# Gating a decoder's expert mixer in rounds of eight tokens instead of four, with single one-hot tiles and another order of ACT and DVE

## The chip, the cores and the metric

The kernel runs on one core of a Trainium2 chip. The metric is the device time of one execution in microseconds (us), as the median of several runs. The engines are TensorE (PE, whose weight loads are listed apart as PEld), VectorE (DVE), ScalarE (ACT), GpSimd (POOL) and SyncE (SP, which here issues the weight transfers). Each engine works through its own queue in order; work on different engines is tied by semaphores.

## The reference

Two decoder layers on 256 tokens of width 1024. Each layer has a token mixer (two kinds of attention, left out here) and a retrieval over 16384 single-neuron experts, and the change is in the second. A token has 8 heads of 16 chosen experts; an expert's index is a pair (i, j) of two 128-way indices.

```python
def expert_block(args):
    tb, eb, gb = args                 # tokens, chosen experts, gates
    act = gelu(einsum('td,ted->te', tb, expert_u[eb]))
    return einsum('te,ted->td', gb * act, expert_v[eb])
```

The kernel doesn't gather the experts. It computes the activations of all 16384 for all tokens, multiplies them by a dense matrix of gates (zero for experts that a token did not choose), and multiplies the result by all of expert_v.

## The kernel before, in words

Everything is in fp32 or in pairs of fp32r halves: a weight block of 128 x 1024 (512 KB) is fetched by SP (`fetch`), ACT rounds it to `hi` (line 90), DVE takes the rest `lo` (line 91), and a product is three matmuls (lines 119 to 121). Blocks come in one fixed order (`plan`). `weights` hands out block n and has block n + 2 cut on the spot (`ahead`); `hi`, `lo` and the raw blocks have three buffers each. The order of instructions in each queue is that of the program text, written out by hand.

A layer's expert part (`peer`, line 666) has these stages. First come queries, scores and the top-16 selection, with 48 of the 128 projections by expert_u beside them (M_PRE = 48, tile `bufa`: for each j one chunk of 128 i x 256 tokens). The selection leaves for each token, in 128 partitions (8 heads x 16), the two indices and the gate cut in three bf16 parts; the tiles are `tT` (lines 953 to 963). Then comes the gating stage, and last `sum_b` (line 155), which multiplies all 128 gated chunks by expert_v; `lhs` cuts a chunk into two halves for it (lines 715 and 716).

The gating stage (lines 723 to 756) does two things together: the other 80 projections (tile `bufb`), and the dense gates. For a token, a one-hot tile compares the i index with 0..127, another the j index (`one_hots`, line 769, against the constant `iotax`); the second is multiplied by the three gate parts (`gated`, line 778). Three matmuls a token then sum a 128 x 128 matrix of gates in PSUM (`dense`, line 788). Tiles hold tokens in adjacent pairs. A round has TB = 4 tokens: four DVE instructions for one-hots, twelve matmuls into one PSUM bank. `apply` (line 791) multiplies these gates into the chunks that are already there: on DVE into `bufa` (line 795) and the J - 48 projected chunks of `bufb` (line 797), and then ACT copies the gates of the chunks still to come into `bufb` (line 799). A later projection J finds gates for the tokens of earlier rounds in its chunk: ACT puts their Gelu into a tile `g` (line 751), that of the other tokens straight into the chunk (line 753), and DVE multiplies `g` in (line 755, "g product" below).

There are 64 rounds and one more, with one or two projections each, so that 80 are done by the end. Within a round the text has: the one-hots of the next round, the projection (with the cut of a later block by ACT and DVE), the gated one-hots of the next round, `apply` for the round before, `dense` for this one, g and Gelu. One-hots and gated one-hots have two buffers, save the j one-hots with one.

At the start of the kernel, 14 matmuls on a constant tile `ones` run while x is fetched (lines 281 to 285). After the first projections of layer 0, thirty small matmuls on `iotax` write a bank that nobody reads (lines 401 to 407). `norm_t` squares x on ACT into the tile `hT[0]` as scratch (lines 213 to 215), in four pieces of 512 columns, scales an identity to `diag` (line 243), and cuts the transposed result into `hT` on ACT (line 251) and DVE (line 252).

Of the kernel before, what the change touches and what calls it, by code (L numbers as in the profile page):

```python
# [9 lines left out]
F32 = mybir.dt.float32  # L10
F32R = mybir.dt.float32r
BF = mybir.dt.bfloat16
U32 = mybir.dt.uint32
AF = mybir.ActivationFunctionType
OP = mybir.AluOpType
# [7 lines left out]
S = 256  # L23
# [8 lines left out]
NCAND = sum(RUNS)  # L32

M_PRE = 48
TB = 4
WARM = 14
NB = S // TB
TAIL = 2
# [7 lines left out]
class Kern:  # L46
# [209 lines left out]
    def build(self):  # L256
        nc, tc, i = self.nc, self.tc, self.i
        with ExitStack() as st:
# [19 lines left out]
            self.gains = const.tile([128, 2, self.depth, KT], F32, name="gains")  # L278
            nc.gpsimd.dma_start(self.gains, i["norm_g"][:, :, 0:self.depth])

            ones = const.tile([128, 128], F32, name="ones")
            nc.vector.memset(ones, 1.0)
            ps = self.bank("ps")
            for _ in range(WARM):
                nc.tensor.matmul(ps[:, 0:128], ones, ones, start=True, stop=True)
            self.iotab = const.tile([128, TOPK], BF, name="iotab")
            self.iotax = const.tile([128, TB // 2, 128, 2], BF, name="iotax")
            self.starts = const.tile([128, 2, 16], BF, name="starts")
            for l in range(self.depth):
                self.mixer(l)  # L290
# [25 lines left out]
    def constants(self, pool):  # L316

        nc, i = self.nc, self.i
        iota = pool.tile([128, 128], F32, name="iota")
        nc.gpsimd.dma_start(iota, i["c_iota"])  # L320
        s32 = pool.tile([128, 2, 16], F32, name="s32")
        nc.gpsimd.dma_start(s32, i["c_runs"])
        rel = pool.tile([33, 5], F32, name="rel")
        oh = pool.tile([33, 384], F32, name="oh")
        nc.gpsimd.dma_start(oh, i["c_bucket"])
        flip = pool.tile([128, 128], F32, name="flip")
        nc.gpsimd.dma_start(flip, i["c_flip"])
        nc.vector.memset(rel, 0.0)
        nc.gpsimd.dma_start(rel[0:32, 0:4], i["rel_bias"])
        nc.vector.memset(rel[32:33, :], 1.0)  # L330
        yield
        ps = self.bank("acc")
        nc.tensor.matmul(ps[0:5, 0:384], rel, oh, start=True, stop=True)
        er = pool.tile([5, 384], F32, name="er")
        nc.vector.tensor_scalar(er, ps[0:5, 0:384], -1.0, None, op0=OP.mult)
        nc.vector.tensor_copy(self.iotab, iota[:, :TOPK])
        for q in range(TB // 2):
            nc.vector.tensor_copy(self.iotax[:, q], iota[:, :, None].to_broadcast([128, 128, 2]))
        nc.vector.tensor_copy(self.starts, s32)
        erow = self.dram.tile([5, 384], F32, name="erow")  # L340
        nc.gpsimd.dma_start(erow, er)

        tr = pool.tile([128, 5, S], F32, name="tr")
        nc.gpsimd.dma_start(tr, bass.AP(tensor=erow.tensor, offset=erow.offset, ap=[[1, 128], [384, 5], [1, S]]))
        yield
        ts = pool.tile([128, 5, S], F32, name="ts")
        for h in range(5):
            ps = self.bank("acc")[:, :S]
            nc.tensor.matmul(ps, flip, tr[:, h], start=True, stop=True)
            nc.scalar.activation(ts[:, h], ps, AF.Copy)  # L350
        self.table = self.dram.tile([128, 5, S], F32, name="table")
        nc.gpsimd.dma_start(self.table, ts)
        yield

    def mixer(self, l):
        nc, tc, i = self.nc, self.tc, self.i
        lam_init = 0.8 - 0.6 * math.exp(-0.3 * l)
        with tc.tile_pool(name="mix", bufs=1) as mp, tc.tile_pool(name="att", bufs=1) as ap, ExitStack() as first:
# [39 lines left out]
                    nc.vector.tensor_scalar(nlam, nlam, -lam_init, None, op0=OP.add)  # L398
            first.close()
            self.ahead(self.used + 3)  # L400
            if l == 0:
                ps = self.bank("acc")
                a = self.iotax[:, 0].rearrange("p n t -> p (n t)")
                b = self.iotax[:, 1].rearrange("p n t -> p (n t)")
                for x, y in ((a[:, :128], b[:, :128]), (a[:, ::2], b[:, :128]), (a[:, :128], b[:, ::2])):
                    for _ in range(10):
                        nc.tensor.matmul(ps[:, :128], x, y, start=True, stop=True)
            tb = mp.tile([128, 5, S], F32, name="tb")
            nc.gpsimd.dma_start(tb, self.table)

# [255 lines left out]
    def peer(self, l):  # L666
        nc, tc, i = self.nc, self.tc, self.i
        with ExitStack() as st:
            sm = st.enter_context(tc.tile_pool(name="sm", bufs=1))
            pa = st.enter_context(tc.tile_pool(name="bufa", bufs=1))  # L670
            tT = [sm.tile([128, S], BF, name=f"tT{q}") for q in range(2)] + [sm.tile([128, S // 2, 3, 2], BF, name="gp")]
            bufa = pa.tile([128, M_PRE, S], F32, name="bufa")
            with tc.tile_pool(name="topk", bufs=1) as tk:
                self.norm_t(tk, self.gains[:, 1, l])
# [48 lines left out]
            with tc.tile_pool(name="wp", bufs=1) as wp:  # L723

                J = M_PRE
                hots = [self.gated(wp, 0, tT, self.one_hots(wp, 0, tT))]
                dense = []
                for b in range(NB + 1):
                    want = M_PRE + -(-(b + 1) * (NJ - M_PRE) // (NB + 1))
                    done = False  # L730
                    while J < want or not done:
                        if not done and b + 1 < NB:
                            hot = self.one_hots(wp, b + 1, tT)
                        if b == NB and not done:
                            self.apply(dense.pop(0), b - 1, bufa, bufb, J)
                            lhs(0)
                            done = True
                        ps = self.proj("uT", l, J) if J < want else None
                        if not done:
                            if b + 1 < NB:  # L740
                                hots.append(self.gated(wp, b + 1, tT, hot))
                            if b >= 1:
                                self.apply(dense.pop(0), b - 1, bufa, bufb, J)
                            if b < NB:
                                dense.append(self.dense(hots.pop(0)))
                            done = True
                        if ps is not None:
                            t0 = max(b, 0) * TB
                            if t0:
                                g = self.ring(wp, "g", [128, S], F32, 1)  # L750
                                nc.scalar.activation(g[:, :t0], ps[:, :t0], AF.Gelu)  # L751
                            if t0 < S:
                                nc.scalar.activation(chunk(J)[:, t0:], ps[:, t0:], AF.Gelu)  # L753
                            if t0:
                                nc.vector.tensor_mul(chunk(J)[:, :t0], chunk(J)[:, :t0], g[:, :t0])  # L755
                            J += 1
# [2 lines left out]
            cuts += [vq.tile([128, 2, S], F32R, name=f"cut{q}") for q in range(2, 4)]  # L759
            self.sum_b(NJ, ("v", l), lhs)  # L760

    def one_hots(self, sm, b, tT):

        nc = self.nc
        ts = slice(b * TB, (b + 1) * TB)
        shp = [128, TB // 2, 128, 2]
        o = [self.ring(sm, f"oh{q}", shp, BF, 2 - q) for q in range(2)]
        for q in range(2):
            nc.vector.tensor_tensor(o[q], self.iotax, tT[q][:, ts].rearrange("p (a b) -> p a b", b=2)[:, :, None].to_broadcast(shp),  # L769
                                    op=OP.is_equal)  # L770
        return o

    def gated(self, sm, b, tT, hot):

        og = self.ring(sm, "ohG", [128, TB // 2, 3, 128, 2], BF, 2)
        for a in range(TB // 2):
            shp = [128, 3, 128, 2]
            self.nc.vector.tensor_tensor(og[:, a], hot[1][:, a, None].to_broadcast(shp),  # L778
                                         tT[2][:, b * TB // 2 + a, :, None].to_broadcast(shp), op=OP.mult)
        return hot[0], og  # L780

    def dense(self, hots):

        oa, og = hots
        ps = self.bank("acc").rearrange("p (t c) -> p t c", c=128)
        for t in range(TB):
            for k in range(3):
                self.nc.tensor.matmul(ps[:, t], oa[:, t // 2, :, t % 2], og[:, t // 2, k, :, t % 2], start=k == 0, stop=k == 2)  # L788
        return ps

    def apply(self, ps, b, bufa, bufb, J):
        nc = self.nc
        ts = slice(b * TB, (b + 1) * TB)
        pv = ps.rearrange("p t c -> p c t")
        nc.vector.tensor_mul(bufa[:, :, ts], pv[:, :M_PRE], bufa[:, :, ts])  # L795
        if J > M_PRE:
            nc.vector.tensor_mul(bufb[:, :J - M_PRE, ts], pv[:, M_PRE:J], bufb[:, :J - M_PRE, ts])  # L797
        if J < NJ:
            nc.scalar.activation(bufb[:, J - M_PRE:, ts], pv[:, J:], AF.Copy)  # L799

    def score(self, tk, sk, q, u):

# [24 lines left out]
    def select(self, tk, tT):  # L827
# [119 lines left out]
        for tt in both:  # L947
# [2 lines left out]
                                     e[:, tt * PH:(tt + 1) * PH].rearrange("p h k -> p (h k)"))):  # L950
                nc.tensor.transpose(ps[:, q * 128:(q + 1) * 128], src, self.ident)
            yield None
            ts = slice(tt * 128, (tt + 1) * 128)
            for q in range(2):
                nc.scalar.activation(tT[q][:, ts], ps[:, q * 128:(q + 1) * 128], AF.Copy)

            rest = self.ring(tk, "rest", [128, 128], F32, 2)
            parts = [tT[2][:, tt * 64:(tt + 1) * 64, k] for k in range(3)]
            pg, r2 = [v.rearrange("p (a b) -> p a b", b=2) for v in (ps[:, 256:384], rest)]
            nc.scalar.activation(parts[0], pg, AF.Copy)  # L960
            nc.vector.tensor_sub(r2, pg, parts[0])
            nc.scalar.activation(parts[1], r2, AF.Copy)
            nc.vector.tensor_sub(parts[2], r2, parts[1])

# [79 lines left out]
```

## Time and profile before

| | us |
|---|---|
| median of 3 runs | 2120.43 |
| lowest, highest | 2120.34, 2125.4 |
| profiled execution, its own time | 2122.72 |
| its span, first to last instruction | 2120.6 |
| PE busy in the span | 2059.1 |
| DVE busy | 1479.6 |
| ACT busy | 1059.7 |

The span is what the trace covers; the profiled execution's own time lies 2.1 us above it. Busy time of an engine is the time in which it had an instruction in work. Matmuls are pipelined, one begins before the last has ended, so PE's pace is read from distances between starts. [...]

### The profile page before, as it was taken

Reading aid. Unit: us, or ns where it says so; the run is one execution under the profiler, and the core shown is the slowest. Engines: PE = TensorE matmul, PEld = TensorE weight load, DVE = VectorE, ACT = ScalarE, POOL = GpSimd, SP = SyncE. Lnnn points to the kernel's source line nnn. Section 1 sums busy time; section 2 is a strip of 40 time slices with the busy share of each in tenths; the row PEclk is TensorE's granted clock in tenths of the full one; section 3 lists DMA queues with packets and bytes.
Section 4 is the critical chain, followed back from the end, with each engine's and each line's share of the span. In section 5 each row is a group of like instructions: output and inputs, shape, how many; then the busy total and the mean of one; then the engine's idle time right before and its main releaser. Section 6 shows DMA issues by size and latency. Waiting matters only on the chain.

```text
span 2120.6 us, 37332 instructions
## 1 busy us (share of the span) xinstructions
PE 2059.1 (97%) x14594; PEld 1879.0 (89%) x14594; DVE 1479.6 (70%) x3255; ACT 1059.7 (50%) x1964; POOL 28.0 (1%) x50
## 2 busy tenths in 40 slices
PE   9999999999999999999999999999999999999998
PEld 8998999998888788888899989999888887888886
DVE  4667798777888655555566668887788885555555
ACT  5665546443333444444466655564433334444444
POOL 2000000000000000000010000000000000000000
PEclk9999999999999999999999999999999999999999
DMA  7455566544444555555555455665444445555564
GB/s 224 144 152 168 160 186 192 162 138 133 137 133 134 171 189 189 189 189 188 189 167 157 153 169 163 189 189 150 140 130 139 130 140 176 189 189 189 188 188 152
DMA packets 97393, 352.76 MB, mean 166 GB/s; under 512 B 11152, under 2 KB 11317, under 8 KB 97216
## 3 DMA queue, kind: packets, MB, share of 16 engines
q1 hardware_dynamic: 95472, 345.68, 52.4%
q0 software_dynamic: 1456, 4.18, 0.7%
q8 instruction: 114, 1.87, 0.4%
q14 instruction: 63, 0.52, 0.1%
q10 hardware_dynamic: 288, 0.52, 0.1%
HBM read 348.62 MB, written 1.71 MB: 165 GB/s over the span
## 4 chain that ended last, share of the span: by engine, by line
PE 71%; DVE 17%; ACT 8%; issue 3%; DMA 0%; POOL 0%; ACTq 0%; POOLq 0%; SPq 0%
PE acc L152 36%; PE ps L119 10%; PE ps L121 10%; PE ps L120 10%; DVE lo L91 7%; DVE ohG L778 5%; ACT hi L90 5%; ACT g L751 2%; DVE bufa L795 1%; DVE oh L769 1%; DVE bufb L797 1%; ACT bufb L753 1%; PE ps L152 1%; PE acc L788 1%; PE acc L806 1%
## 5 line engine op out<-in xcount | busy, mean ns | idle before, releaser
L91 DVE TENSOR_TENSOR lo<-raw,hi 128x1024 fp32r<-128x1024 f32 (+1 forms) x656 | 802.0, 1224 | 487.2 <-ACT hi L90 483.5
L90 ACT ACTIVATE hi<-raw 128x1024 fp32r<-128x1024 f32 (+1 forms) x656 | 696.9, 1063 | 394.7 <-PE acc L152 386.1
L119 PE MATMUL ps<-hT,hi 128*128 128x256 f32 x2784 | 799.8, 287 | 0.0
L121 PE MATMUL ps<-hT,lo 128*128 128x256 f32 x2784 | 783.8, 282 | 13.7 <-DVE lo L91 13.6
L120 PE MATMUL ps<-hT,hi 128*128 128x256 f32 x2784 | 784.4, 282 | 0.0
L152 PE MATMUL acc<-hi,cut 128*128 128x512 f32 x2048 | 562.5, 396 | 6.0 <-ACT cut L715 6.0
L121 PEld LDWEIGHTS ps<-hT,lo 128*128 128x128 f32 x2784 | 524.9, 189 | 19.7 <-DVE lo L91 19.1
L119 PEld LDWEIGHTS ps<-hT,hi 128*128 128x128 f32 x2784 | 523.2, 188 | 3.9 <-issue 3.7
L120 PEld LDWEIGHTS ps<-hT,hi 128*128 128x128 f32 x2784 | 523.7, 188 | 0.3
L152 PEld LDWEIGHTS acc<-hi,cut 128*128 128x128 f32 x2048 | 386.1, 189 | 96.6 <-ACT cut L715 6.4
L152 PE MATMUL acc<-lo,cut 128*128 128x512 f32 x1024 | 322.3, 395 | 0.0
L152 PEld LDWEIGHTS acc<-lo,cut 128*128 128x128 f32 x1024 | 192.8, 188 | 45.9
L799 ACT ACTIVATE bufb<-acc 128x312 f32<-128x312 f32 (+42 forms) x128 | 38.9, 304 | 370.6 <-DVE bufb L797 311.6
L788 PE MATMUL acc<-ohG,oh 128*128 128x128 bf16 x1536 | 117.2, 219 | 26.1 <-DVE ohG L778 26.1
L788 PEld LDWEIGHTS <-oh 128*128 128x128 bf16 x1536 | 95.3, 97 | 41.0 <-issue 30.1
L778 DVE TENSOR_TENSOR ohG<-oh,gp 128x768 bf16<-128x768 bf16 x256 | 130.7, 552 | 0.1
L755 DVE TENSOR_TENSOR bufb<-bufb,g 128x4 f32<-128x4 f32 (+25 forms) x156 | 45.6, 293 | 74.7 <-ACT g L751 74.7
L769 DVE TENSOR_TENSOR oh<-iotax,tT 128x512 bf16<-128x512 bf16 x256 | 96.5, 419 | 0.0
L690 ACT ACTIVATE bufa<-ps 128x256 f32<-128x256 f32 x96 | 37.1, 386 | 112.1 <-PE ps L121 112.0
L716 DVE TENSOR_TENSOR cut<-bufb,cut 128x256 fp32r<-128x256 f32 x160 | 66.9, 418 | 0.0
L715 ACT ACTIVATE cut<-bufb 128x256 fp32r<-128x256 f32 x160 | 64.3, 402 | 0.0
L753 ACT ACTIVATE bufb<-ps 128x240 f32<-128x240 f32 (+47 forms) x158 | 46.0, 291 | 7.5 <-PE ps L121 7.5
(240 smaller groups left out, 1413.1 us busy)
## 6 DMA issues: line engine op xcount, KB each, us to landing
raw<-uT SPq DMA_DIRECT2D x256, 512.0 KB, 3.7
raw<-expert_v SPq DMA_DIRECT2D x256, 512.0 KB, 3.6
raw<-wA SPq DMA_DIRECT2D x64, 512.0 KB, 3.6
raw<-wQ SPq DMA_DIRECT2D x32, 512.0 KB, 3.7
raw<-wV SPq DMA_DIRECT2D x16, 516.0 KB, 4.3
raw<-wO SPq DMA_DIRECT2D x16, 512.0 KB, 3.8
raw<-w_out SPq DMA_DIRECT2D x16, 512.0 KB, 4.0
tb<-table POOLq DMA_DIRECT2D x2, 640.0 KB, 5.8
```

The lines of the kernel that those rows point to most:

```text
L90: nc.scalar.activation(hi[:, :w], raw[:, :w], AF.Copy)
L91: nc.vector.tensor_sub(lo[:, :w], raw[:, :w], hi[:, :w].bitcast(F32))
L119: self.nc.tensor.matmul(ps, ah, bh, start=first and q == 0, stop=False)
L120: self.nc.tensor.matmul(ps, ah, bl, start=False, stop=False)
L121: self.nc.tensor.matmul(ps, al, bh, start=False, stop=last and q == n - 1)
L152: self.nc.tensor.matmul(ps[:, :width], a, b[:, g * width:(g + 1) * width], start=first and n == 0, stop=last and n == 2)
L715: nc.scalar.activation(a[:, 0], chunk(n), AF.Copy)
L716: nc.vector.tensor_sub(a[:, 1], chunk(n), a[:, 0].bitcast(F32))
L753: nc.scalar.activation(chunk(J)[:, t0:], ps[:, t0:], AF.Gelu)
L769: nc.vector.tensor_tensor(o[q], self.iotax, tT[q][:, ts].rearrange("p (a b) -> p a b", b=2)[:, :, None].to_broadcast(shp), op=OP.is_equal)
L778: self.nc.vector.tensor_tensor(og[:, a], hot[1][:, a, None].to_broadcast(shp), tT[2][:, b * TB // 2 + a, :, None].to_broadcast(shp), op=OP ...
L788: self.nc.tensor.matmul(ps[:, t], oa[:, t // 2, :, t % 2], og[:, t // 2, k, :, t % 2], start=k == 0, stop=k == 2)
```

## The change

- Rounds have eight tokens (32 and one more), with two or three projections each. The projections of a round are steps: after the first comes `dense` for this round, after the second `apply` for this round and then the one-hots of the next.
- `one_hots` makes both kinds of index one-hots for eight tokens in one DVE instruction of 2048 elements a partition, and the gated ones in one of 3072; both tiles have one buffer. The index and gate tiles `tT` are laid out by rounds for it; ACT and DVE write them in the selection with as many instructions as before.
- `dense` is 24 matmuls in a row, into two banks.
- `apply` has ACT copy first, for both banks, and then the DVE products.
- `ones` is no tile of its own but the first 128 columns of `hT[0]`; `iotax` has one copy instead of two; the thirty matmuls on it are gone.

```diff
-TB = 4
+TB = 8
...
-            ones = const.tile([128, 128], F32, name="ones")
+            ones = self.hT[0].rearrange("p k t -> p (k t)")[:, :128].bitcast(F32)
...
-            if l == 0:
-                ps = self.bank("acc")
-                a = self.iotax[:, 0].rearrange("p n t -> p (n t)")
-                b = self.iotax[:, 1].rearrange("p n t -> p (n t)")
-                for x, y in ((a[:, :128], b[:, :128]), (a[:, ::2], b[:, :128]), (a[:, :128], b[:, ::2])):
-                    for _ in range(10):
-                        nc.tensor.matmul(ps[:, :128], x, y, start=True, stop=True)
...
-                hots = [self.gated(wp, 0, tT, self.one_hots(wp, 0, tT))]
-                dense = []
+                hots = self.one_hots(wp, 0, tT)
                 for b in range(NB + 1):
                     want = M_PRE + -(-(b + 1) * (NJ - M_PRE) // (NB + 1))
...
+                    step = 0
+                    while J < want or step < 2:
+                        ps = self.proj("uT", l, J) if J < want else None
+                        if b < NB and step == 0:
+                            dense = self.dense(*hots)
+                        if b < NB and step == 1:
+                            self.apply(dense, b, bufa, bufb, J)
+                            if b + 1 < NB:
+                                hots = self.one_hots(wp, b + 1, tT)
+                        if b == NB and step == 0:
                             lhs(0)
...
+                        step += 1
                         if ps is not None:
-                            t0 = max(b, 0) * TB
+                            t0 = min(b + (step > 1), NB) * TB
...
+        oh = self.ring(wp, "oh", [128, 2, TB // 2, 128, 2], BF, 1)
+        og = self.ring(wp, "ohG", [128, 3, TB // 2, 128, 2], BF, 1)
+        flat = lambda t: t.rearrange("p k a n t -> p (k a n t)")
+        cols = [t[:, b].rearrange("p k t -> p (k t)").rearrange("p (a t) -> p a t", t=2) for t in tT]
+        nc.vector.tensor_tensor(flat(oh), self.iotax.rearrange("p n t -> p (n t)")[:, None].to_broadcast([128, TB, 256]),
+                                cols[0][:, :, None].to_broadcast([128, TB, 128, 2]), op=OP.is_equal)
+        nc.vector.tensor_tensor(flat(og), flat(oh)[:, None, TB * 128:].to_broadcast([128, 3, TB * 128]),
+                                cols[1][:, :, None].to_broadcast([128, 3 * TB // 2, 128, 2]), op=OP.mult)
+        return oh, og
...
+        banks = [self.bank("acc").rearrange("p (t c) -> p t c", c=128) for _ in range(TB // 4)]
         for t in range(TB):
             for k in range(3):
...
+    def apply(self, banks, b, bufa, bufb, J):
+        nc = self.nc
+        tiles = [(slice(b * TB + 4 * n, b * TB + 4 * n + 4), ps.rearrange("p t c -> p c t"))
+                 for n, ps in enumerate(banks)]
         if J < NJ:
-            nc.scalar.activation(bufb[:, J - M_PRE:, ts], pv[:, J:], AF.Copy)
+            for ts, pv in tiles:
+                nc.scalar.activation(bufb[:, J - M_PRE:, ts], pv[:, J:], AF.Copy)
+        for ts, pv in tiles:
+            nc.vector.tensor_mul(bufa[:, :, ts], pv[:, :M_PRE], bufa[:, :, ts])
+            if J > M_PRE:
+                nc.vector.tensor_mul(bufb[:, :J - M_PRE, ts], pv[:, M_PRE:J], bufb[:, :J - M_PRE, ts])
```

## Rows read from the trace of the kernel before

**Rows 1.** The page's first part: busy us (share of the span), instructions.

```profile
PE 2059.1 (97%) x14594; PEld 1879.0 (89%) x14594; DVE 1479.6 (70%) x3255; ACT 1059.7 (50%) x1964; POOL 28.0 (1%) x50
```

**Rows 2.** Window, gating stage: length; PE, PEld, DVE, ACT, POOL busy; clock; DMA.

```profile
397.00:705.31 308.31, 285.37 (x2667) 274.78 (x2665) 248.73 (x535) 120.49 (x300) 0.00 (x0) 1.00 0.45 136
```

**Rows 3.** Waits of the whole run: who for whom, us in total, times, longest.

```profile
ACT bufb L799 <- DVE bufb L797: 311.6, 107, 3.7
...
PE acc L788 <- DVE ohG L778: 26.1, 60, 0.6
...
PE acc L152 <- ACT cut L715: 6.0, 2, 3.0
```

**Rows 4.** Timeline: two projections' ends (ACT), two early dense groups (PE); start, length.

```profile
388.73 0.39 ACT L690 ACTIVATE bufa<-ps 128x256 f32<-128x256 f32 x1 [0.30 <-PE ps L121]
...
391.56 0.39 ACT L690 ACTIVATE bufa<-ps 128x256 f32<-128x256 f32 x1 [1.49 <-PE ps L121]
...
407.04 0.86 PE L788 MATMUL acc<-ohG,oh 128*128 128x128 bf16 x12
...
410.63 0.86 PE L788 MATMUL acc<-ohG,oh 128*128 128x128 bf16 x12
```

**Rows 5.** Timeline of DVE in a late round of layer 0.

```profile
671.40 0.38 DVE L755 TENSOR_TENSOR bufb<-bufb,g 128x224 f32<-128x224 f32 x1
671.70 0.75 DVE L769 TENSOR_TENSOR oh<-iotax,tT 128x512 bf16<-128x512 bf16 x2
672.37 1.22 DVE L91 TENSOR_TENSOR lo<-raw,hi 128x1024 fp32r<-128x1024 f32 x1
673.51 1.02 DVE L778 TENSOR_TENSOR ohG<-oh,gp 128x768 bf16<-128x768 bf16 x2
674.44 0.35 DVE L795 TENSOR_TENSOR bufa<-acc,bufa 128x192 f32<-128x192 f32 x1
674.71 0.45 DVE L797 TENSOR_TENSOR bufb<-acc,bufb 128x284 f32<-128x284 f32 x1
```

**Rows 6.** Timeline of ACT in an early round (first row) and the late one.

```profile
404.71 0.43 ACT L799 ACTIVATE bufb<-acc 128x312 f32<-128x312 f32 x1 [2.57 <-DVE bufb L797]
...
675.19 0.20 ACT L799 ACTIVATE bufb<-acc 128x36 f32<-128x36 f32 x1 [3.68 <-DVE bufb L797]
675.29 0.36 ACT L751 ACTIVATE g<-ps 128x228 f32<-128x228 f32 x1
675.53 0.20 ACT L753 ACTIVATE bufb<-ps 128x28 f32<-128x28 f32 x1
675.61 1.07 ACT L90 ACTIVATE hi<-raw 128x1024 fp32r<-128x1024 f32 x1
```

**Rows 7.** Timeline of PE: the thirty matmuls on iotax, and the length of one.

```profile
40.30 1.87 PE L407 MATMUL acc<-iotax 128*128 128x128 bf16 x30
...
L407 PE MATMUL acc<-iotax x30: 218/219/230, 40.3 to 41.9; 128*128 128x128 bf16 x30
```

**Rows 8.** DVE's one-hot instructions: ns shortest/median/longest, first and last start, shape.

```profile
L778 DVE TENSOR_TENSOR ohG<-oh,gp x256: 549/552/559, 394.9 to 1747.0; 128x768 bf16<-128x768 bf16 x128
...
L769 DVE TENSOR_TENSOR oh<-iotax,tT x256: 416/419/423, 394.1 to 1745.0; 128x512 bf16<-128x512 bf16 x128
```

**Rows 9.** Windows after the waits for the first cut, layers 0 and 1.

```profile
705.00:709.00 4.00, 3.69 (x16) 3.04 (x17) 3.22 (x5) 3.59 (x7) 0.00 (x0) 1.00 0.10 25
1755.00:1759.00 4.00, 4.00 (x12) 3.12 (x12) 3.03 (x4) 2.41 (x5) 0.00 (x0) 0.57 0.34 101
```

**Rows 10.** Timeline of the kernel's start: PE, ACT, DVE.

```profile
1.08 4.92 PE L285 MATMUL ps<-ones 128*128 128x128 f32 x28 [1.08 <-DVE ones L282]
...
3.27 0.63 ACT L214 ACTIVATE hT<-x 128x512 fp32r<-128x512 f32 x1 [1.25 <-DMA x<-x]
...
8.63 0.29 DVE L243 TENSOR_SCALAR diag<-ident,rs_y 128x128 f32<-128x128 f32 x1
...
12.09 3.22 DVE L252 SCALAR_TENSOR_TENSOR hT<-acc,gains,hT 128x256 fp32r<-128x256 f32 x8
```

More of the change, by code (lines that the diff above doesn't have):

```diff
@@ L286, in build @@
             self.iotab = const.tile([128, TOPK], BF, name="iotab")
-            self.iotax = const.tile([128, TB // 2, 128, 2], BF, name="iotax")
+            self.iotax = const.tile([128, 128, 2], BF, name="iotax")
             self.starts = const.tile([128, 2, 16], BF, name="starts")
@@ L336, in constants @@
         nc.vector.tensor_copy(self.iotab, iota[:, :TOPK])
-        for q in range(TB // 2):
-            nc.vector.tensor_copy(self.iotax[:, q], iota[:, :, None].to_broadcast([128, 128, 2]))
+        nc.vector.tensor_copy(self.iotax, iota[:, :, None].to_broadcast([128, 128, 2]))
         nc.vector.tensor_copy(self.starts, s32)
@@ L670, in peer @@
             pa = st.enter_context(tc.tile_pool(name="bufa", bufs=1))
-            tT = [sm.tile([128, S], BF, name=f"tT{q}") for q in range(2)] + [sm.tile([128, S // 2, 3, 2], BF, name="gp")]
+            tT = [sm.tile([128, NB, n, TB], BF, name=f"tT{n}") for n in (2, 3)]
             bufa = pa.tile([128, M_PRE, S], F32, name="bufa")
@@ L725, in peer @@
                 J = M_PRE
-                hots = [self.gated(wp, 0, tT, self.one_hots(wp, 0, tT))]
-                dense = []
+                hots = self.one_hots(wp, 0, tT)
                 for b in range(NB + 1):
                     want = M_PRE + -(-(b + 1) * (NJ - M_PRE) // (NB + 1))
[L730 to L735, printed above, removed]
-                            lhs(0)
[L737 to L746, printed above, removed]
+                    step = 0
[8 more added lines that the diff above has]
+                        if b == NB and step == 0:
+                            lhs(0)
+                        step += 1
                         if ps is not None:
-                            t0 = max(b, 0) * TB
+                            t0 = min(b + (step > 1), NB) * TB
                             if t0:
@@ L760, in peer, with one_hots @@
             self.sum_b(NJ, ("v", l), lhs)
-    def one_hots(self, sm, b, tT):
+    def one_hots(self, wp, b, tT):
         nc = self.nc
[L765 to L785, printed above, removed]
+        oh = self.ring(wp, "oh", [128, 2, TB // 2, 128, 2], BF, 1)
@@ L786, in dense @@
+        return oh, og
+    def dense(self, oh, og):
+        banks = [self.bank("acc").rearrange("p (t c) -> p t c", c=128) for _ in range(TB // 4)]
         for t in range(TB):
             for k in range(3):
-                self.nc.tensor.matmul(ps[:, t], oa[:, t // 2, :, t % 2], og[:, t // 2, k, :, t % 2], start=k == 0, stop=k == 2)
-        return ps
-    def apply(self, ps, b, bufa, bufb, J):
+                self.nc.tensor.matmul(banks[t // 4][:, t % 4], oh[:, 0, t // 2, :, t % 2], og[:, k, t // 2, :, t % 2],
+                                      start=k == 0, stop=k == 2)
+        return banks
@@ L792, in apply @@
+    def apply(self, banks, b, bufa, bufb, J):
         nc = self.nc
[L793 to L797, printed above, removed]
-        if J < NJ:
-            nc.scalar.activation(bufb[:, J - M_PRE:, ts], pv[:, J:], AF.Copy)
+        tiles = [(slice(b * TB + 4 * n, b * TB + 4 * n + 4), ps.rearrange("p t c -> p c t"))
+                 for n, ps in enumerate(banks)]
+        if J < NJ:
+            for ts, pv in tiles:
[4 more added lines that the diff above has]
+                nc.vector.tensor_mul(bufb[:, :J - M_PRE, ts], pv[:, M_PRE:J], bufb[:, :J - M_PRE, ts])
@@ L952, in select @@
             yield None
-            ts = slice(tt * 128, (tt + 1) * 128)
+            bs = slice(tt * NB // 2, (tt + 1) * NB // 2)
+            pv = ps[:, 0:384].rearrange("p (q b t) -> p q b t", q=3, t=TB)
             for q in range(2):
-                nc.scalar.activation(tT[q][:, ts], ps[:, q * 128:(q + 1) * 128], AF.Copy)
+                nc.scalar.activation(tT[0][:, bs, q], pv[:, q], AF.Copy)
             rest = self.ring(tk, "rest", [128, 128], F32, 2)
[L958 to L961, printed above, removed]
+            parts = [tT[1][:, bs, k] for k in range(3)]
+            r2 = rest.rearrange("p (b t) -> p b t", t=TB)
+            nc.scalar.activation(parts[0], pv[:, 2], AF.Copy)
+            nc.vector.tensor_sub(r2, pv[:, 2], parts[0])
             nc.scalar.activation(parts[1], r2, AF.Copy)
```

## Prediction

> **What bounds the kernel now.** I read the page first: TensorE (PE) is busy for 2059.1 of the span's 2120.6 us [rows 1]. That looks as if only fewer matmuls could help, but it is an average over stages, so the next view is the windows over the stretch that the change rewrites: the gating stage, from its first dense matmul to the first matmul of expert_v. It lasts 308.31 us in layer 0, and layer 1 repeats it; PE is busy there for 285.4 and DVE for 248.7 [rows 2]. Three quarters of PE's idle time in the span (2 x 22.9 of 61.5 us) lie in these two stretches, and no engine is full in them.
>
> The waits say why [rows 3]. ACT's copy of its share of the gates waits 311.6 us in all for DVE's product on bufb; PE's dense matmuls wait 26.1 us for the gated one-hots; and at the end of the stage PE waits about 3.0 us, once a layer, for the first cut. Is PE itself slow where it doesn't wait? Two consecutive projections with nothing else on PE end 391.56 - 388.73 = 2.83 us apart [rows 4]. Early in the stage, where the one-hots are still ahead, dense group follows dense group after 410.63 - 407.04 = 3.59 us, one projection and twelve dense matmuls [rows 4]; so twelve cost 0.76 us. A late round with one projection shows what rules in its place [rows 5, 6]: DVE runs lo, gated one-hots, bufa product, bufb product back to back; only after the bufb product can ACT copy (at 675.19, after 3.68 us of waiting), and behind that copy in ACT's queue stand g, the Gelu and the hi cut that DVE needs next. The two engines take turns, and a round takes longer than the 3.59 us that PE needs.
>
> **The change part by part.** *PE's work in the stage* stays: 79 projections after the first dense group, and 768 dense matmuls a layer. One dense matmul costs about (1.87 - 0.22)/29 = 0.057 us (30 like ones take 1.87, the last with its tail) [rows 7]; so 24 at once cost 0.76 + 12 x 0.057 = 1.44 us. If PE never waits, the stage takes 32 x 1.44 + 79 x 2.83 = 46.1 + 223.6 = 269.7 us: 38.6 less than 308.3, 77.2 for two layers. That is the ceiling; the question is whether DVE and ACT keep up.
>
> *The one-hots.* Per eight tokens, eight DVE instructions become two with as many elements. From 512 elements (419 ns) to 768 (552) is 133 ns for 256, 0.52 ns each [rows 8], so 2048 take 419 + 1536 x 0.52 = 1.22 us and 3072 take 552 + 2304 x 0.52 = 1.75; successive DVE instructions overlap by some 0.08, so 1.14 + 1.67 = 2.81. Before it was 2 x (0.67 + 0.93) = 3.20 [rows 5]. Bounds: 2.81 (the slope holds) to 3.20 (merging saves nothing). I take 2.81: the operands keep adjacent pairs and the type.
>
> *A late round with two projections*, counted from T0, when ACT can read its first projection. ACT: g 0.24, Gelu 0.08, hi 1.07 [rows 6], done at 1.39. DVE then does lo from 1.43 to 2.57. PE's dense group ends by 1.44, so ACT's two copies end at the latest at 1.44 + 2 x 0.43 = 2.30 (0.43 is the longest, early copy; late ones take 0.20) [rows 6]. So the products, next on DVE, find the copies done: **this wait goes, and its successor has 0.27 us to spare**. Products: 2 x (0.27 + 0.36) = 1.26 (a late bufb product lasts 0.45, less the overlap) [rows 5], to 3.83. One-hots of the next round: 2.81 + 0.08, to 6.72. PE wants them at 2 x 2.83 + 1.44 = 7.10, or somewhat before, since matmuls overlap. So PE just doesn't wait. Behind the one-hots DVE still owes one g product (0.30) and one lo (1.14), which end by 8.2; that lo belongs to a projection that starts a round later. DVE's whole round is 2 x 1.14 + 2 x 0.30 + 1.26 + 2.81 = 6.95 of 7.10. A round with three projections gives PE 9.93 and DVE 8.39. Of the 33 rounds 14 have three projections, and the last has no gating, so 18 a layer are the tight ones. For these I add 1 us in all (0 if the walk is exact; 36 x 0.3 = 11 if the one-hots cost 3.20 and the margin is gone).
>
> *The single one-hot tiles* make the next compare wait for the dense matmuls that read them (over at 1.44); DVE comes to it at 3.83, so this costs nothing, and would only where DVE had no products to do first. Behind that compare DVE's queue holds the gated product, g product and lo above. *The DMAs* of weights are issued at the same places in program order; a block every 3.5 us in place of 3.9 is asked for, and the projections before this stage take one every 2.83 [rows 4]. Cost nothing. *The end of the stage*: two projections follow the last gating where one did, 5.7 us that cover products and cuts; the 3.0 us a layer are in the 77.2 already.
>
> [...] *The 30 matmuls on iotax* go: 29 x 0.057 = 1.65 us, with PE the bound of that stage (between 0 and 1.87) [rows 7].
>
> *The alias of ones.* The norm's first Square writes over ones, so it waits for the warm-up matmuls, which end at 1.08 + 4.92 = 6.00; before it began at 3.27 [rows 10], 2.73 later. The second diag (8.63) then comes about 2 us later, but DVE reached the norm's low parts only at 12.09, behind two weight cuts [rows 10], and I find it there 0.3 later. Cost 0.3, bounds 0 (all hidden) and 2.7 (none). PE's gap after the warm-up grows from about 1 to about 3 us, as long as the gap that once let the clock fall and once not [rows 9]; a fall would add up to 1.7, within these ends. [...]
>
> *Sum.* The profiled execution took 2122.72, its span 2120.6 and 2.1 around it; the median of the three runs is 2120.43. Against its own time: 2122.72 - 77.2 - 1.65 - 1.7 + 0.3 + 1 = 2043.5. Against the median, without the fall: 2120.43 - 77.2 - 1.65 + 0.3 + 1 = 2042.9. Forecast **2043**, faster by 3.7%.
>
> **Rivals.** *A, the wait changes hands* (0.14): DVE now stands behind ACT's copies, or a lo slips in front of the one-hots, and PE waits in the tight rounds. For it speaks the thin margin; against it the 0.27 us between copies and products. It costs 36 us for each us per round beyond the margin of 0.2: 0.5 gives 2054, a whole lo (1.14) 2077. I say 2050 to 2077. [...]
>
> *B, only the merging counts* (0.08), so the change doesn't do what its words say of the order: the copy wasn't what held the loop, and DVE stays at 248.7/308.3 = 0.81 of the time. Then 32 x 0.39 = 12.5 us less DVE work a layer gives 15.5 a layer: 2120.4 - 31 - 1.4 = 2088. Against it speaks that ACT's and DVE's waits close in a ring in each round [rows 5, 6].
>
> *C, the long one-hot instructions run at one element a step* (0.04), half the rate. The place is the two DVE instructions; the price 1.04 ns an element: 2.20 + 3.27 = 5.47 a round. With products and g products at half of their late sizes, DVE needs 3.54 + 5.47 in a tight round and 4.86 + 5.47 in the others: 18 x 9.01 + 14 x 10.33 + 5.7 = 312.5 a layer, and with some 0.2 of waiting a round 319: 2120 + 21 - 1 = **2140, slower**. It decides from a pair cost of about 5.1 us (with that waiting). Against it: at 0.52 ns the same pattern shows the double rate now [rows 8].
>
> **How the numbers follow.** Forecast 0.72, A 0.14, B 0.08, C 0.04, and 0.02 that gains and losses cancel. The forecast's own range is 2039 (nothing added for tight rounds, nothing at the start) to 2054 (one-hots at 3.20). Eight in ten need half of A as well: 2038 to 2062. A measurement here tells 0.3%, some 6 us, from no change. Faster 0.94, same 0.02, slower 0.04.
>
> **What would show it.** Right: the stage at about 270 us a layer; two long one-hot instructions at 1.22 and 1.75 us; no wait of ACT's copy for DVE; dense groups that don't wait; no gap before the first expert_v matmul; the first Square at 6.0. Wrong: dense matmuls that wait for the gated one-hots in tight rounds (A), DVE waits on the copies (A), a stage near 293 us with copies still late (B), one-hots of 2.2 and 3.3 us (C).

## The result, and the profile after

The changed kernel takes 2046.66 us (median of 4 runs, 2046.48 to 2047.25) against 2121.36 for the kernel before beside it. The ratio is 0.9645, 95% interval 0.9628 to 0.9662. The profiled execution took 2046.84, its span 2045.1.

First the page's busy line, which answers to [rows 1], and the windows over the gating stage of the changed kernel, layer 0 and layer 1 (length; PE, PEld, DVE, ACT, POOL busy; the clock granted to PE, as a share of the full one; DMA share and GB/s), which answer to [rows 2]:

```profile
PE 2027.8 (99%) x14564; PEld 1867.6 (91%) x14564; DVE 1447.9 (71%) x2872; ACT 1060.2 (52%) x1962; POOL 28.0 (1%) x50
...
399.50:669.60 270.10, 270.10 (x2666) 268.71 (x2664) 234.45 (x350) 123.03 (x300) 0.00 (x0) 1.00 0.52 155
1410.04:1680.20 270.16, 270.16 (x2665) 268.76 (x2664) 234.50 (x350) 123.02 (x300) 0.00 (x0) 1.00 0.51 155
```

By these windows the stage has shrunk by 38.2 us in layer 0 and 38.1 in layer 1, and PE is busy in all of it. Between the two stages nothing changed: 740.42 us before, 1410.04 - 669.60 = 740.44 after. Behind the second stage the span is 1.7 us shorter, as much as the fall of the clock [rows 9] took, 4 us at 0.57 (4 x 0.43); here the clock reads 1.00 from 1680.2 to 1690. And the stage of layer 0 begins 2.5 us later than before, though 30 matmuls are gone ahead of it. So 76.3 and 1.7 were gained and 2.5 lost: 75.5, the difference of the spans.

A tight round of the changed kernel late in layer 0, on the timeline of PE, DVE and ACT (start, length):

```profile
642.61 1.55 PE L767 MATMUL acc<-ohG,oh 128*128 128x128 bf16 x24
649.72 1.55 PE L767 MATMUL acc<-ohG,oh 128*128 128x128 bf16 x24
659.65 1.55 PE L767 MATMUL acc<-ohG,oh 128*128 128x128 bf16 x24
...
644.23 1.23 DVE L91 TENSOR_TENSOR lo<-raw,hi 128x1024 fp32r<-128x1024 f32 x1 [0.63 <-ACT hi L90]
645.37 0.35 DVE L779 TENSOR_TENSOR bufa<-acc,bufa 128x192 f32<-128x192 f32 x1
645.64 0.45 DVE L781 TENSOR_TENSOR bufb<-acc,bufb 128x288 f32<-128x288 f32 x1
646.00 0.35 DVE L779 TENSOR_TENSOR bufa<-acc,bufa 128x192 f32<-128x192 f32 x1
646.27 0.45 DVE L781 TENSOR_TENSOR bufb<-acc,bufb 128x288 f32<-128x288 f32 x1
646.63 1.21 DVE L756 TENSOR_TENSOR oh<-iotax,tT 128x2048 bf16<-128x2048 bf16 x1
647.88 1.76 DVE L758 TENSOR_TENSOR ohG<-oh,tT 128x3072 bf16<-128x3072 bf16 x1
649.56 0.40 DVE L741 TENSOR_TENSOR bufb<-bufb,g 128x240 f32<-128x240 f32 x1
...
644.09 0.32 ACT L777 ACTIVATE bufb<-acc 128x32 f32<-128x32 f32 x2
```

A round with two projections takes 649.72 - 642.61 = 7.11 us, one with three 9.93. ACT's copies end at 644.41, a microsecond before the first product; the one-hots end at 649.64, and PE takes them up at 649.72. The two long instructions last 1.21 and 1.76 us. In [rows 5, 6] the copy followed the product; here it precedes it, and no engine holds up PE. No dense group of the run waits, and the first matmul of expert_v follows the last projection without a gap.

The start of the changed kernel, which answers to [rows 10], on the timeline of PE, ACT and DVE, and two of its windows:

```profile
1.08 6.23 PE L285 MATMUL ps<-hT 128*128 128x128 f32 x28 [1.08 <-DVE hT L282]
10.40 5.46 PE L246 MATMUL acc<-diag,x 128*128 128x128 f32 x32 [3.09 <-DVE diag L243]
15.62 0.72 PE L152 MATMUL ps<-hi,hT 128*128 128x344 f32 x3
...
7.35 0.63 ACT L214 ACTIVATE hT<-x 128x512 fp32r<-128x512 f32 x1 [2.57 <-PE ps L285]
...
11.58 0.29 DVE L243 TENSOR_SCALAR diag<-ident,rs_y 128x128 f32<-128x128 f32 x1
15.12 3.02 DVE L252 SCALAR_TENSOR_TENSOR hT<-acc,gains,hT 128x256 fp32r<-128x256 f32 x7 [0.97 <-ACT hT L251]
...
11.00:12.00 1.00, 1.00 (x6) 1.00 (x6) 0.80 (x4) 0.81 (x1) 1.00 (x3) 0.50 0.00 0
12.00:13.00 1.00, 1.00 (x7) 1.00 (x6) 1.00 (x2) 0.00 (x0) 1.00 (x3) 0.50 0.15 3
```

The Square does wait for the warm-up, which took 6.23 us here. PE then idles for 3.09 us, the granted clock is 0.50 from 11 to 13 us, and the transposes take 5.46 us. In the kernel before, at 1.00 from 7 to 12 us, they took 3.87 and began 3.24 us earlier:

```profile
7.16 3.87 PE L246 MATMUL acc<-diag,x 128*128 128x128 f32 x32 [1.16 <-DVE diag L243]
```

DVE comes to the low parts at 15.12, not at 12.4, after 0.97 us of waiting for ACT's part of `hT`, which is taken from the transposes.

### The profile page after: what moved, and what is told of

Read it like the earlier page. It is cut to its first block, busy times and chain, and to the rows that moved or that the text cites. A ratio compares the mean times of both kernels' runs of the same rounds, so it can differ in the third digit from the quotient of the medians.

```text
span 2045.1 us, 36789 instructions
## 1 busy us (share of the span) xinstructions
PE 2027.8 (99%) x14564; PEld 1867.6 (91%) x14564; DVE 1447.9 (71%) x2872; ACT 1060.2 (52%) x1962; POOL 28.0 (1%) x50
## 4 chain that ended last, share of the span: by engine, by line
PE 98%; issue 1%; DMA 1%; DVE 0%; ACT 0%; POOL 0%; POOLq 0%; ACTq 0%
PE acc L152 37%; PE ps L119 17%; PE ps L120 17%; PE ps L121 17%; PE acc L767 4%; PE ps L152 1%; PE acc L788 1%; PE acc L246 1%; PE acc L634 1%; PE ps L564 0%; PE acc L576 0%; PE ps L285 0%; DMA tr<-erow 0%; PE acc L651 0%; DMA lam<-diff_lambda 0%
## 5 line engine op out<-in xcount | busy, mean ns | idle before, releaser
L737 ACT ACTIVATE g<-ps 128x8 f32<-128x8 f32 (+31 forms) x158 | 44.4, 281 | 294.5 <-PE ps L121 280.2
L758 DVE TENSOR_TENSOR ohG<-oh,tT 128x3072 bf16<-128x3072 bf16 x64 | 112.5, 1758 | 2.2
L767 PE MATMUL acc<-ohG,oh 128*128 128x128 bf16 x1536 | 99.3, 219 | 0.0
L767 PEld LDWEIGHTS <-oh 128*128 128x128 bf16 x1536 | 88.3, 97 | 2.9
L756 DVE TENSOR_TENSOR oh<-iotax,tT 128x2048 bf16<-128x2048 bf16 x64 | 77.8, 1215 | 0.0
L741 DVE TENSOR_TENSOR bufb<-bufb,g 128x8 f32<-128x8 f32 (+31 forms) x158 | 46.1, 292 | 15.5 <-ACT g L737 15.5
L779 DVE TENSOR_TENSOR bufa<-acc,bufa 128x192 f32<-128x192 f32 x128 | 44.7, 349 | 0.0
```

The lines of the kernel that those rows point to most:

```text
L756: nc.vector.tensor_tensor(flat(oh), self.iotax.rearrange("p n t -> p (n t)")[:, None].to_broadcast([128, TB, 256]), cols[0][:, :, None].to ...
L758: nc.vector.tensor_tensor(flat(og), flat(oh)[:, None, TB * 128:].to_broadcast([128, 3, TB * 128]), cols[1][:, :, None].to_broadcast([128, ...
L767: self.nc.tensor.matmul(banks[t // 4][:, t % 4], oh[:, 0, t // 2, :, t % 2], og[:, k, t // 2, :, t % 2], start=k == 0, stop=k == 2)
```

## The experiments

The theory after the result: the stage before was paced by a ring, that is, a chain of instructions on two engines in which each waits for the one before it, and the first for the last: bufb product, ACT's copy, g, Gelu, hi, lo, gated one-hots, bufa product, and back to the bufb product. In [rows 5, 6] it can be walked: from 674.71 the product takes 0.48 with the hand-over, copy 0.10, g 0.24, Gelu 0.08, hi and hand-over 1.10, lo 1.14, gated one-hots 0.94, bufa product 0.27, in all 4.35 us, against PE's 3.59. Each number is the distance to the next start. The round is as long: from lo at 672.37 to the next round's, on the timeline of the kernel before,

```profile
676.71 1.23 DVE L91 TENSOR_TENSOR lo<-raw,hi 128x1024 fp32r<-128x1024 f32 x1
```

it is 4.34 us. The rivals: only the work saved on DVE counts (B of the prediction), or only the length of the round. The change made several edits at once; the first five runs undo some of them or take one alone. Each ratio below is to the kernel before on the same chip.

**Eight tokens, DVE first again.**

```diff
-        if J < NJ:
-            for ts, pv in tiles:
-                nc.scalar.activation(bufb[:, J - M_PRE:, ts], pv[:, J:], AF.Copy)
         for ts, pv in tiles:
...
+        if J < NJ:
+            for ts, pv in tiles:
+                nc.scalar.activation(bufb[:, J - M_PRE:, ts], pv[:, J:], AF.Copy)
```

> Eight tokens a round as in the change, but apply has the DVE products first and ACT's two copies last, as before. If the order of the two is what the gain needs, the ring between ACT and DVE closes again and the stage goes back towards 308 us a layer: 2100 to 2120. If the spacing of a round of eight is enough by itself (products end 3.8 us after the round's first projection, ACT's next g comes 4.2 after it, so a copy behind the products still ends in time), nothing changes: 2045 to 2049, gating stage 270 us, dense groups that don't wait.

Measured 2044.87 us, ratio 0.9632 (0.9619 to 0.9645). The waits of the whole run, and the window over the stage of layer 0:

```profile
ACT bufb L781 <- DVE bufb L778: 129.4, 100, 2.0
...
397.45:667.60 270.15, 270.15 (x2666) 268.76 (x2665) 234.45 (x350) 129.74 (x300) 0.00 (x0) 1.00 0.52 155
```

ACT waits for DVE's product again, 100 times and 129.4 us in all, and it costs nothing. The new order isn't needed at eight tokens; and the wait that led the list in [rows 3] wasn't a cost by itself, but by what stood behind it.

**Four tokens, ACT first: the kernel before with the order alone.**

```diff
+        if J < NJ:
+            nc.scalar.activation(bufb[:, J - M_PRE:, ts], pv[:, J:], AF.Copy)
         nc.vector.tensor_mul(bufa[:, :, ts], pv[:, :M_PRE], bufa[:, :, ts])
...
-        if J < NJ:
-            nc.scalar.activation(bufb[:, J - M_PRE:, ts], pv[:, J:], AF.Copy)
```

> The kernel before, four tokens a round, with one edit: in apply ACT copies before the DVE products. If the order carries the gain, ACT no longer waits for the bufb product, a round with one projection takes 3.6 to 3.7 us in place of 4.35, the stage 275 us a layer: 2050 to 2066. If rounds of eight and the merged one-hots carry it, the order alone gives nothing: 2115 to 2121.

Measured 2047.99, ratio 0.9645 (0.9631 to 0.966), a little under the 2050 to 2066 that I expected of the order. In the stage, two lines swapped give 36 of the 38 us a layer that the whole change gives. That the whole times agree as well is chance: this kernel keeps the thirty matmuls and a tile of its own for `ones`, and begins its stage some 2.6 us earlier than the changed one. The window over the stage of layer 0, and two late rounds of DVE (its oh and lo, between g product and ohG, are left out):

```profile
396.82:669.07 272.25, 272.25 (x2667) 269.39 (x2665) 243.20 (x537) 123.03 (x301) 0.00 (x0) 1.00 0.51 154
...
658.25 1.02 DVE L778 TENSOR_TENSOR ohG<-oh,gp 128x768 bf16<-128x768 bf16 x2
659.18 0.35 DVE L797 TENSOR_TENSOR bufa<-acc,bufa 128x192 f32<-128x192 f32 x1
659.45 0.47 DVE L799 TENSOR_TENSOR bufb<-acc,bufb 128x304 f32<-128x304 f32 x1
659.83 0.40 DVE L755 TENSOR_TENSOR bufb<-bufb,g 128x244 f32<-128x244 f32 x1
...
661.96 1.02 DVE L778 TENSOR_TENSOR ohG<-oh,gp 128x768 bf16<-128x768 bf16 x2
```

PE is busy throughout, and a round takes 661.96 - 658.25 = 3.71 us, all of it DVE work, in place of 4.35. No g product waits for g in these two rounds. That the stage is 2.1 us longer than with eight tokens is PE's part: by the prediction's sizes 64 dense groups of 0.76 against 32 of 1.44 would be 2.6.

**One-hots in eight instructions again.**

```diff
-        nc.vector.tensor_tensor(flat(oh), ..., op=OP.is_equal)
-        nc.vector.tensor_tensor(flat(og), ..., op=OP.mult)
+        x = self.iotax.rearrange("p n t -> p (n t)")[:, None]
+        for c in range(0, TB, 2):
+            nc.vector.tensor_tensor(flat(oh)[:, c * 256:(c + 2) * 256], x.to_broadcast([128, 2, 256]),
+                                    cols[0][:, c:c + 2, None].to_broadcast([128, 2, 128, 2]), op=OP.is_equal)
+        gp = tT[1][:, b].rearrange("p k (a t) -> p k a t", t=2)
+        for a in range(TB // 2):
+            shp = [128, 3, 128, 2]
+            nc.vector.tensor_tensor(og[:, :, a], oh[:, 1, a, None].to_broadcast(shp),
+                                    gp[:, :, a, None].to_broadcast(shp), op=OP.mult)
```

> The changed kernel with the one-hots of a round in eight DVE instructions again (four of 512 and four of 768 elements), 3.20 us a round in place of 2.81. In the tight rounds the one-hots now end 0.08 us (late) to 0.7 us (early) before PE wants them, so 0.39 more costs nothing early and up to 0.3 late: 2047 to 2052. If the merging carries the gain (rival B), most of it goes: 2065 or more.

Measured 2045.20, ratio 0.9634 (0.962 to 0.9647), stage 270.16, below the 2047 to 2052 that I expected. Rival B falls. The run doesn't price the margin, though: DVE's one-hots of a late tight round end at 647.97, after PE has begun its dense group:

```profile
647.76 1.55 PE L772 MATMUL acc<-ohG,oh 128*128 128x128 bf16 x24
...
644.67 1.42 DVE L758 TENSOR_TENSOR oh<-iotax,tT 128x512 bf16<-128x512 bf16 x4
646.01 1.96 DVE L763 TENSOR_TENSOR ohG<-oh,tT 128x768 bf16<-128x768 bf16 x4
```

With four pieces the first matmuls didn't wait for the last piece. Merging saves DVE 0.29 us a round (3.01 from 646.63 to 649.64 above, 3.30 here), and PE began at 649.72, behind the whole.

**Both undone: eight tokens, DVE first, eight instructions.** The edits are the first and the third together.

> The changed kernel with both of its other parts undone: DVE products before ACT's copies, and the one-hots in eight instructions. What is left is the round of eight tokens and the new place of its steps. If each of the two undone parts could go only because the other stayed, the ring or the late one-hots come back: 2060 or more. If the long round is enough by itself: 2043 to 2048, stage 270 us.

Measured 2045.43, ratio 0.9636 (0.9621 to 0.9651), stage 270.16. The round of eight and the new place of its steps are enough.

**The new place of the steps with four tokens, DVE first.**

```diff
-TB = 8
+TB = 4
```

and the first edit.

> The changed program with four tokens a round (TB = 4) and the DVE products before ACT's copy: the new place of the steps without the long round and without the new order. The ring of before was bufb product, copy, g and Gelu, hi, lo, gated one-hots, bufa product: 0.45 + 0.2 + 0.32 + 1.07 + 1.14 + 0.93 + 0.27 = 4.4 us, the round of before. Here it is product, copy, hi, lo, g product: some 3.4 us, under the 3.6 us of PE. If the ring is the cause, 2046 to 2062 with a stage of 272 to 280 us; if eight tokens a round are the cause, 2105 to 2125.

Measured 2048.17, ratio 0.9651 (0.9636 to 0.9665). The waits within the stage of layer 0, and its window:

```profile
ACT bufb L781 <- DVE bufb L778: 73.1, 64, 2.0
...
396.40:668.65 272.25, 272.25 (x2666) 269.39 (x2665) 243.06 (x411) 130.00 (x302) 0.00 (x0) 1.00 0.51 154
```

Copy follows product in all 64 rounds, a round is four tokens long, and the stage is the same as with the order alone. What the new program takes out of the ring is the stretch in which the gated one-hots stood between lo and the products. This run keeps the one-hots merged, but that takes little off the walk: the gated ones of four tokens, in one instruction,

```profile
655.65 0.96 DVE L758 TENSOR_TENSOR ohG<-oh,tT 128x1536 bf16<-128x1536 bf16 x1
```

last 0.96 us where two lasted 1.02 [rows 5], and the ring had 0.76 to lose to PE. So there are two ways to open the ring: the order of copy and product (second run), and the place of the steps (this one). The place of the steps with four tokens and unmerged one-hots wasn't tried, nor the longer round without the new place.

**A dose in the ring.** The Gelu into g done twice, in the kernel before and in the changed one.

```diff
                                 nc.scalar.activation(g[:, :t0], ps[:, :t0], AF.Gelu)
+                                nc.scalar.activation(g[:, :t0], ps[:, :t0], AF.Gelu)
```

> The kernel before, with the Gelu into g done twice (78 short ACT instructions a layer more, 0.06 to 0.28 us each by their spacing, 0.17 in the mean; ACT is idle for 61% of the stage). If the stage is paced by the ring, in which g stands, each of them lengthens its round: 13 us a layer, 26 in all, 2140 to 2152. If the stage is paced by the sum of DVE's work, ACT has room for them and nothing changes: 2120 to 2125.

Measured 2163.07, ratio 1.0184 (1.0169 to 1.02): 39.1 us more, in the direction that the ring gives, and above the 2140 to 2152 that I had for it. The window over the stage of layer 0, 19.2 us longer than before, and two g late in it, on the timeline of ACT:

```profile
396.49:723.99 327.50, 289.16 (x2667) 275.43 (x2665) 248.75 (x535) 141.62 (x377) 0.00 (x0) 1.00 0.43 128
...
663.35 0.23 ACT L800 ACTIVATE bufb<-acc 128x64 f32<-128x64 f32 x1 [2.89 <-DVE bufb L798]
663.47 0.34 ACT L751 ACTIVATE g<-ps 128x208 f32<-128x208 f32 x1
663.84 0.34 ACT L752 ACTIVATE g<-ps 128x208 f32<-128x208 f32 x1
```

The second, into the same tile, begins only when the first has ended (663.81, then 663.84): 0.37 us apart, where I had taken 0.06 to 0.28, 0.17 in the mean, from the spacing of g and a different successor. 39.1 over 156 is 0.25 us each. DVE has no more work than before (248.75), and ACT is idle for more than half of the stage; still, more work on ACT makes it longer.

> The same dose in the changed kernel: g done twice. PE paces the stage there and ACT's g ends well before DVE needs what is behind it, save in the tight rounds, where hi and lo move 0.25 us later late in the stage and the one-hots have 0.08 to 0.7 us to spare: 2046 to 2051. If the ring still ruled in the changed kernel: 2070.

Measured 2048.21 (2046.57 to 2051.16), within what I expected: 4.9 us over the changed kernel beside it (2043.31) and 1.8 over the one on another chip (2046.39). The stage, which the start doesn't touch, tells it better, 1.8 us longer a layer:

```profile
395.62:667.52 271.90, 271.10 (x2665) 269.31 (x2664) 234.01 (x350) 144.98 (x378) 0.00 (x0) 1.00 0.52 154
```

Two dense groups of layer 0 wait, 0.5 us in all. The dose that costs the kernel before 19.2 us a layer costs this one a tenth of that.

**The margin of the tight rounds.** The compare done twice.

```diff
+        nc.vector.tensor_tensor(flat(oh), ..., op=OP.is_equal)
         nc.vector.tensor_tensor(flat(oh), ..., op=OP.is_equal)
```

> The changed kernel with the compare of 2048 elements done twice into the same tile, 1.14 us more on DVE in each round. By my walk of a round the one-hots then come 0.4 to 1.1 us after PE wants them in the 36 tight rounds and still in time in the others: 25 us more (15 to 35), 2060 to 2080, dense groups that wait for ohG. If PE has more slack there than the walk gives it: under 2050.

> The changed kernel itself, unaltered, beside the others on the same chip. Gating stage 270.1 us a layer again. What may move is the start of layer 0: its first projection began between 42.1 and 44.1 us in the profiles of kernels with the same start, by the warm-up's own pace. So 2044 to 2047.

Measured 2080.67, ratio 0.9799 (0.9784 to 0.9814), beside the changed kernel with 2046.39, ratio 0.9639 (0.9626 to 0.9652): 34.3 us for 1.25 us of DVE a round, within the 15 to 35 that I expected, the time itself just past the 2080. The wait of the dense groups within the stage of layer 0, three tight rounds of PE, one early and two late, and DVE's one-hots in the last of them:

```profile
PE acc L769 <- DVE ohG L760: 15.0, 18, 1.2
...
418.06 1.54 PE L769 MATMUL acc<-ohG,oh 128*128 128x128 bf16 x24 [0.50 <-DVE ohG L760]
640.02 1.53 PE L769 MATMUL acc<-ohG,oh 128*128 128x128 bf16 x24 [1.02 <-DVE ohG L760]
648.46 1.54 PE L769 MATMUL acc<-ohG,oh 128*128 128x128 bf16 x24 [1.19 <-DVE ohG L760]
...
644.14 1.21 DVE L756 TENSOR_TENSOR oh<-iotax,tT 128x2048 bf16<-128x2048 bf16 x1
645.39 1.23 DVE L758 TENSOR_TENSOR oh<-iotax,tT 128x2048 bf16<-128x2048 bf16 x1
646.65 1.76 DVE L760 TENSOR_TENSOR ohG<-oh,tT 128x3072 bf16<-128x3072 bf16 x1
648.33 0.38 DVE L741 TENSOR_TENSOR bufb<-bufb,g 128x224 f32<-128x224 f32 x1
```

It waits 18 times a layer: once at the first dense group of the stage, and behind 17 of the 18 tight rounds that the prediction counted; the last of them has no one-hots to make. The rounds with three projections absorb the dose. The wait grows from 0.50 us in the first tight round to 1.2 in the last, of a dose of 1.25. So the changed kernel has over half a us of slack in an early tight round and next to none in a late one: this is the price of rival A.

**The start: ones over hT[1] in place of hT[0].**

```diff
-            ones = self.hT[0].rearrange("p k t -> p (k t)")[:, :128].bitcast(F32)
+            ones = self.hT[1].rearrange("p k t -> p (k t)")[:, :128].bitcast(F32)
```

> The changed kernel, with ones laid over hT[1], which the norm writes only at the end, in place of hT[0]. If the alias is why the first projections begin late, the first Square starts at 3.3 us again, PE's gap after the warm-up shrinks from 3.1 to about 1 us, the clock doesn't fall there, and the run is 3 to 4.5 us shorter: 2042 to 2044. If the alias is hidden as I predicted (0.3 us) and the late start was a matter of the warm-up's own pace in that execution: 2046 to 2047.

Measured 2042.32, ratio 0.962 (0.9607 to 0.9633). Two runs with ones over hT[0] and a stage as long, on the same chip (DVE first, and eight instructions), have 2044.87 and 2045.20: 2.5 to 2.9 us more.

> The changed kernel with ones over hT[1] once more, beside the changed kernel itself on the same chip. By the first run of it 3 to 4 us under the changed kernel: 2042 to 2043, no fall of the clock in the first 16 us.

> The changed kernel once more, for the comparison with ones over hT[1]: 2045 to 2047, PE idle for 3.1 us after the warm-up and then at the lower clock for some us.

Measured 2041.94, ratio 0.9614 (0.96 to 0.9627), and 2043.31, ratio 0.9621 (0.9608 to 0.9634). The difference of these two, run side by side, is 1.4 us, less than the 3 to 4 that I expected, since the changed kernel came out at 2043.31, below the 2045 to 2047 that I had for it; against its 2046.39 on another chip it is 4.4. The transposes on the timeline of PE, with ones over hT[1], and then in the changed kernel beside it:

```profile
7.19 3.87 PE L246 MATMUL acc<-diag,x 128*128 128x128 f32 x32 [0.61 <-DVE diag L243]
```

```profile
10.35 5.46 PE L246 MATMUL acc<-diag,x 128*128 128x128 f32 x32 [3.09 <-DVE diag L243]
```

The first projection of layer 0 begins at 40.35 and 39.97 us in the two profiles with hT[1]. In the nine with hT[0] it begins anywhere from 40.24 (no fall of the clock in the transposes, 3.84 us) to 44.11, with 42.90 in the middle. The clock isn't all of this spread. Before the matmuls of line 348 (349 before) PE waits for a DMA, 0.70 us in the kernel before, 1.29 in the profile of the result, and 0 to 1.75 in the nine. The longest is in the run with the one-hots in eight instructions, where the clock didn't fall in the transposes (3.84) and the first projection came at 42.22 all the same:

```profile
33.70 3.02 PE L348 MATMUL acc<-tr,flip 128*128 128x256 f32 x10 [1.75 <-DMA tr<-erow]
```

What DVE makes for this transfer also comes later when the start is late, so how much of that wait is the alias's is not shown. With the alias the first projection comes 0 to 4 us later in an execution, and the medians of runs on one chip lie 1.4 to 2.9 us higher. Ones over hT[1] is the fastest version found, though the intervals of its ratios overlap with the others'.

## Why the prediction was right, and the term that was off

**The ceiling and the sum** held. I had 269.7 us for the stage if PE never waits; it is 270.1 and never waits. 77.2 us for both layers are 76.3. The missing gap before expert_v, the one fall of the clock behind it (1.7 us, seen as 1.7 at the end of the span) and the 30 matmuls (1.65) came as predicted: with ones over hT[1] the first projection starts at 40.0 to 40.4, 1.6 to 2.0 us earlier than the 41.97 of the profile before. The 1.7 of the sum is the 4 us at 0.57 in place of 1.00 in layer 1 [rows 9]; that it goes with the wait was an estimate, since after as long a wait in layer 0 the clock read 1.00.

**The walk of the tight round** held closely. It gave 7.10 us for PE, measured 7.11; copies done before the products, measured with a microsecond to spare; one-hots of 1.22 and 1.75 us, measured 1.215 and 1.758. One size was off: compare and gated product are 1.25 us apart, not 1.14; the second, which reads what the first wrote, begins at 647.88, after its end at 647.84. So the pair takes 2.93, where the walk had 2.81, and PE wants it some 0.2 us before the 7.10, as the walk had allowed: of 0.38 us to spare 0.08 were left. The allowance of 1 us for 36 tight rounds wasn't needed. The lower end of the range, 2039, is not what its words add up to: without the 1 and the 0.3 the sum against the median is 2041.6.

**The step that failed** is "Cost 0.3" for the alias of ones. It puts the first projection at 41.97 - 1.65 + 0.3 = 40.6; it came at 44.11, 3.5 us later. That is nearly the whole distance from 2043 to 2046.7, since the 0.9 us missing in the stages and the 1 us not needed for the tight rounds cancel; and 3.8 for the alias lies outside its own bounds, 0 to 2.7. That 2046.7 is in the range all the same is luck: the room up to 2054 was meant for slower one-hots. I had put the norm's second diag 2 us later and let the cuts on DVE hide it. The warm-up ended at 7.31 in this execution and at 6.00 in the one before, so the shift was 2.95. The cuts hid nothing: what held DVE's low parts was ACT's part of `hT`, which needs PE's transposes, and these began 3.24 us later, at 10.40. PE's longer gap was followed by a fall of the clock to 0.50, and the transposes took 1.6 us longer; I had named this as up to 1.7 more and left it out of the sum. And PE's wait for the DMA at line 348 grew by 0.6. What followed differs from execution to execution: after gaps of 3.1 us the transposes took 3.84 in three profiles and 5.3 to 6.7 in the six others. So the 1.7 belonged into the sum with a chance.

**The cause** was right in what it named and too narrow in what it credited. I wrote that the wait of copy on product goes and that this frees the stage. The wait is back in the three runs with DVE first (129.4 us in the first of them) without any cost. What ruled was the ring as a whole, 4.35 us against PE's 3.59; the change opens it twice over.

**Rivals.** A stayed a price without a case: 34 us for 1.25, where its rule, 36 us for each us beyond 0.2, gives 38. B fell: the order alone, with no DVE work saved, gives nearly the whole gain in the stage, and one-hots in eight instructions lose none of it. C fell with the two measured lengths.

## What to carry to other kernels

Before an instruction is moved or merged, walk the ring: start at the wait that leads the list, follow each hand-over until you are back, and add up; if the sum is the round, the ring sets the pace. Here either of two ways to open it gave the whole gain, and the bound after it was PE's own work. A wait by itself proves nothing: look at what is queued behind the waiting instruction and who needs it. And scratch that is laid over another tile saved space here at the price of a wait, 2.57 us of ACT for PE; choose a tile that is written late, as hT[1] is here.

## What the runs showed that I had not expected

- ACT waiting 129.4 us for DVE cost nothing, where with the 311.6 us of the same wait 75 us went.
- 156 more short instructions on ACT, which idled for 61% of the stage, made the run 39.1 us longer, 0.25 us each.
- The warm-up of 28 passes took 4.7 to 6.2 us; in the kernel before, its pace rose on the way from 6 passes a us to 10. In those first microseconds the profile's granted clock reads 1.00 all the same. Passes of the same shape, in the transposes, ran at 6 to 7 a us where 0.50 was granted (11 to 13 us, above) and at 10 to 11 at 1.00 (8 to 11 us in the kernel before); so the 1.00 of the first microseconds doesn't fit their pace, and what the clock was there is not shown. Two windows of the kernel before, whose second entry is PE's busy time with its matmul passes, and whose clock is the number before the DMA share:

```profile
3.00:4.00 1.00, 1.00 (x6) 1.00 (x6) 0.00 (x0) 0.73 (x2) 0.00 (x0) 1.00 0.83 241
4.00:5.00 1.00, 1.00 (x10) 1.00 (x9) 0.21 (x1) 0.73 (x2) 0.00 (x0) 1.00 0.86 288
```

- The reader of the long merged instruction waited for the whole: the dense group began at 649.72, the instruction had ended at 649.64. In pieces, the dense group started 0.21 us before the last piece was done.
